# Delta rule: two merge columns moved from behind the early heads into a front pair, and a later ready mark for the conversions

## The chip, the cores and the metric

The kernel runs on one core of one Trainium2 chip. The metric is the device time of one execution in microseconds (us). The time before is 2187.66 us, the median of three runs between 2187.45 and 2188.29. A program on one core has TensorE (matrix products, with its weight loads), VectorE (DVE), ScalarE (ACT), GpSimd (POOL) and SyncE (SP, which issues most DMAs).

## The reference, cut to what matters

One layer of an encoder works on 640 tokens (512 of a prompt, 8 times 16 of samples), in float32:

```
z = x @ w_in              # q|k|v|forget|gate (FoX), q|k|v|decay|beta|gate (delta rule), m_a, m_b
branch A: forgetting attention, 8 heads of 128        -> y_a = (o_a * silu(gate_a)) @ w_out_fox
branch B: causal convolution of width 4 and SiLU on q|k|v, l2-normalised q and k,
          gated delta rule, 8 heads of 128, in chunks -> y_b = (o_b * silu(gate_b)) @ w_out_gdn
h  = (sigmoid(m_a) * y_a + sigmoid(m_b) * y_b) @ w_out
x1 = layer_norm(alpha * x + h)
out = x1 + sigmoid(x1 @ w_pl_gate) * rms_norm(p @ w_pl_proj)
```

The change concerns the projection for `m_a` and `m_b`, here called merge columns: 32 blocks of 128 output channels, each 2048 deep, of which only the hyperbolic tangent is stored until the end (tensor `md`). It also concerns the delta rule of branch B, which runs head after head.

## The kernel before, in words

Every weight block of 128 channels is a "column". Weights and activations are split into a high and a low float32r part (tiles `wh`, `wl`, `xh`, `xl`), and a product is three matmuls: high by high, high by low, low by high. The 640 tokens are cut into two halves of 320.

There are two ways to compute a column. `column` (its matmuls in `mm6`, lines 396 and 397) runs 16 steps along the depth, each with six matmuls of 320, so 96 matmuls; `mcol` (line 1547 applies the tanh, line 1548 stores to `md`) does this for one merge column. `pair` (matmuls at line 474) takes two columns at once with seven products of half the depth, each of 8 steps of three matmuls: 168 matmuls for two columns. It needs sums of the weight blocks, made on DVE in `w_sum` (line 319), sums of the activations that are made once in `front`, and additions of the products (line 483 and in the closing functions such as `merges`, lines 1410 and 1414).

The program has stages: `front` (first columns, then `PAIRS` pairs: gates, values, `FRONT` merge columns, q and k of the heads in `APART`), `phase_fox` (attention, with the three merge columns that are left between and behind its heads, and the projection of p), `phase_gdn` (the delta rule), and `tail`.

In `phase_gdn` the main flow is, for every head h, three columns q, v, k, each evacuated by `strip_evac` (lines 844 to 849), and then `FILL[h]` merge columns. The fills carry no dependency on the head; they keep TensorE at work while the delta rule of earlier heads goes on. The last of them (two of `FILL[7]`) are written out separately, behind them follow four plain columns of `w_out_fox` and four half-depth pairs, then `until(gdone == 7)`, and `tail`, whose first column needs the output of head 7 as its last operand (`nop[15]`).

The order of all instructions is fixed at build time. The main flow calls `tick` once per step of six matmuls, and `tick` lets the side "lanes" take a step; a lane is a queue of generators, run one after another. A `yield n` in a lane means that it goes on after n ticks and not before the modelled engine has ended what it emitted. Some lanes step at every second tick only (`every = 2`, set to 1 when the columns of head 7 are done). `until(cond)` ticks without emitting any column until `cond` holds. The engines then take their instructions strictly in this order, and semaphores make them wait where the model was wrong. The lanes of the delta rule are:

- `conv`: `conv_silu` (line 852): four taps (ACT line 860, DVE line 863), tanh (ACT line 869), and the last two operations on DVE (lines 873 and 878), after which `self.ready[c] = h` is set. Before the last two it waits for `done[c]`, so as not to overwrite what an earlier head still reads.
- `work`: `gdn` (line 883). Its first instruction waits in the order for `chdone >= h - 3` and for `ready` of all three; it then emits transposes on TensorE (lines 895 to 898 and 908), a load on SP (line 888), and more.
- `blocks`: `gdn_blocks`, the inversion of 32 by 32 blocks: two DMAs through memory (`lanes`, line 980), then 62 dependent operations on DVE (lines 986 and 988).
- `feeds`, and `chunks`: `gdn_chunks` with `gdn_pro` and `gdn_dec`, the recurrence itself. It begins with the load of the state on SP (line 1014) and ends with the store of the final state (line 1195). Only one head at a time is in this lane.
- `ends`: `gdn_out` (the output transposes at lines 1051 and 1055), which sets `gdone`. At the start of the stage this lane also holds `scale_e`, which must end before `gdn` of head 0 may start.
- `sums`: sums of later weights (DMAs at lines 291 and 301, GpSimd at line 295).

The host lays the weight blocks out in the order of use, from the same constants `FRONT` and `FILL`.

Of the kernel before, what the change touches and what calls it, by code (L numbers as in the profile page):

```python
# [52 lines left out]
class Kernel:  # L53
# [5 lines left out]


    PIECES = 5
    FRONT = 32 - 5 - 7
    NG = 8
    PAIR0, PAIRS = 6, NG + 2 + FRONT // 2 + 2
    BETWEEN = 6,
    APART = 3, 6
    FILL = 1, 1, 1, 1, 1, 0, 0, 4
    PLAIN = 4
    GATES = 6
    FREE = 0.5  # L70
# [781 lines left out]
    def conv_silu(self, strip, ct, h, c, dst):  # L852

        nc, tp = self.nc, self.taps
        nc.gpsimd.tensor_copy(out=self.tails[:, ct, 0:3], in_=strip[:, NPT:NPT + 3])
        nc.gpsimd.tensor_copy(
            out=self.tails[:, ct, 3:27].rearrange("p (b r) -> p b r", r=3),
            in_=strip[:, NPT + 3:SW].rearrange("p (b r) -> p b r", r=19)[:, :, 16:19])
        y = self.zt([P, SW], "cy")
        nc.scalar.mul(y[:, 0:CV], strip[:, 0:CV], tp[:, 4 * ct:4 * ct + 1])  # L860
        yield -1
        for i in range(1, 4):
            nc.vector.scalar_tensor_tensor(out=y[:, 0:CV], in0=strip[:, i:i + CV],
                                           scalar=tp[:, 4 * ct + i:4 * ct + i + 1], in1=y[:, 0:CV],
                                           op0=ALU.mult, op1=ALU.add)
            yield -1
        self.untapped -= 1
        th = self.zt([P, SW], "cth")
        nc.scalar.activation(th[:, 0:CV], y[:, 0:CV], AF.Tanh)
        yield 2  # L870
        while self.done[c] < h - (2, 1, 3)[c]:
            yield
        nc.vector.scalar_tensor_tensor(out=dst[:, 0:NPT], in0=th[:, 0:NPT], scalar=1.0, in1=y[:, 0:NPT],
                                       op0=ALU.add, op1=ALU.mult)

        def dv(x):
            return x[:, NPT + 3:SW].rearrange("p (b r) -> p b r", r=19)[:, :, 0:16]
        nc.vector.scalar_tensor_tensor(out=dst[:, NPT:T].rearrange("p (b r) -> p b r", r=16), in0=dv(th), scalar=1.0,
                                       in1=dv(y), op0=ALU.add, op1=ALU.mult)
        self.ready[c] = h  # L880
        yield

    def gdn(self, h, kq, v):
        nc, cb = self.nc, self.cb
# [376 lines left out]
    def front(self, work):  # L1261
# [70 lines left out]
        def parts(src, hi, lo):  # L1332
            nc.scalar.copy(out=hi, in_=src)
            nc.vector.tensor_tensor(out=lo, in0=src, in1=hi.bitcast(F32), op=ALU.subtract)
# [86 lines left out]
        def heads(x, hf, z, u=None):  # L1421
# [8 lines left out]

            def close(h=self.APART[n - self.NG - 2 - self.FRONT // 2]):
                if x == 0:
                    nc.scalar.mul(o, o, FOX_SCALE)
                nc.sync.dma_start(out=self.qkd[h, x], in_=m[x])
                if x:
                    nc.sync.dma_start(out=self.o["fk"][h], in_=m[x])
# [10 lines left out]
        for n in range(self.PAIRS):  # L1447
# [3 lines left out]
            def back(i, k):  # L1451
# [14 lines left out]
                if i == 6:  # L1466
                    hi, lo = self.op[2 * k]
                    parts(tiles[k // 3][:, (k % 3) * HALF:(k % 3 + 1) * HALF], hi[:, xb], lo[:, xb])
            self.pair(xf, gates if n < self.NG else vals if n < self.NG + 2 else merges if n < self.NG + 2 + self.FRONT // 2
                      else heads, back)  # L1470
            if n < self.NG:
                self.ng += 2
            elif self.NG + 2 <= n < self.NG + 2 + self.FRONT // 2:
                self.nm += 2
# [76 lines left out]
    def phase_gdn(self, conv, work):  # L1551
# [20 lines left out]
        for h in range(H):  # L1572
# [13 lines left out]
            work["gens"].append(self.gdn(h, kq, v))  # L1586
            for _ in range(self.FILL[h] if h < 7 else self.FILL[7] - 2):
                self.mcol("sg")
# [750 lines left out]
def _layout(a):  # L2339
# [13 lines left out]
          for g in range(1)]  # L2353
    nf = Kernel.FRONT
    m_ = iter(m[nf + 3:])
# [13 lines left out]
    for h in range(H):  # L2369
        bl += [gq[h], gv[h], gk[h]]  # L2370
        bl += [next(m_) for _ in range(Kernel.FILL[h])]
    for n in ("w_out_fox", "w_out_gdn"):
# [78 lines left out]
```

## Time and profile before

| | us |
|---|---|
| median of three runs | 2187.66 (2187.45 to 2188.29) |
| the profiled execution | 2189.74 |
| its span, first to last instruction | 2188.0 |
| TensorE busy | 2162.9 |
| VectorE / ScalarE / GpSimd busy | 1526.9 / 1001.8 / 393.4 |
| mean granted TensorE clock | 0.996 |

The profile is one execution, read by the hardware profiler. Busy time of an engine sums the time in which at least one of its instructions ran; a matmul row gives a duration of about 310 ns, but matmuls overlap, so the pace is read from the start of one to the start of the next. "Idle before" is the time that an engine stood still ahead of an instruction, and the name behind the arrow is what released it. `SPq` is the queue of DMA issues on SP. The chain that ended last follows the work back from the last instruction. By the trace, `phase_gdn` reaches its first evacuation at 960.1 us and its last stores of half-depth pairs a little before 1660 us.

### The profile page before, as it was taken

To read this page: it belongs to the slowest core of one execution; us is meant where nothing else is said; L and a number is where in the kernel's file an instruction comes from. 1 tells how busy PE (TensorE), PEld (TensorE's weight loads), DVE (VectorE), ACT (ScalarE), POOL (GpSimd) and SP (SyncE) were. 2 spreads that over 40 slices of the span, in tenths; PEclk is the share of its full clock that TensorE was granted. 3 is DMA by queue.
4 is the path that set the end of the run, shared out by engine and by line. 5 is a ranking of instruction groups with operands and counts; after the bars stand their busy time and mean duration, and the time that the engine had idled before them with its cause. 6 is when DMAs were issued, how large, how long until landed. Compare 5 with 4: busy or idle time off the path is not lost.

```text
span 2188.0 us, 41906 instructions
## 1 busy us (share of the span) xinstructions
PE 2162.9 (99%) x15510; PEld 2094.9 (96%) x15510; DVE 1526.9 (70%) x3158; ACT 1001.8 (46%) x2198; POOL 393.4 (18%) x599
## 2 busy tenths in 40 slices
PE   9999999999999999999999999999999999999998
PEld 7799999999999999999999999988999999999998
DVE  6877786767765445575767567766657787789987
ACT  4344443444443333445555666554344343354544
POOL 0023232322200111013334333331000000011100
PEclk9999999999999999999999999999999999999999
DMA  6356556665549888579888888877467656574465
GB/s 233 103 184 198 188 185 204 203 202 183 185 157 339 279 277 293 199 254 284 199 195 194 184 193 189 188 174 205 143 235 255 222 164 208 195 272 135 148 229 172
DMA packets 236781, 451.07 MB, mean 206 GB/s; under 512 B 35416, under 2 KB 119000, under 8 KB 236576
## 3 DMA queue, kind: packets, MB, share of 16 engines
q1 hardware_dynamic: 220448, 419.02, 58.9%
q0 software_dynamic: 16128, 29.37, 8.2%
q8 instruction: 122, 2.00, 0.4%
q14 instruction: 83, 0.68, 0.1%
HBM read 353.22 MB, written 95.07 MB: 205 GB/s over the span
## 4 chain that ended last, share of the span: by engine, by line
PE 91%; DVE 3%; DMA 3%; ACT 1%; issue 1%; SPq 0%; POOL 0%; DVEq 0%; ACTq 0%
PE g L474 40%; PE g L396 20%; PE g L397 20%; PE g L440 2%; PE s L956 1%; PE s L778 1%; PE s L693 1%; PE s L734 1%; ACT wh L329 1%; DMA lanes<-ld 1%; PE s L1102 1%; PE s L440 0%; PE s L788 0%; DVE sx L986 0%; DVE sx L988 0%
## 5 line engine op out<-in xcount | busy, mean ns | idle before, releaser
L329 ACT CAST wh<-wr 128x512 fp32r<-128x512 f32 x630 | 384.9, 619 | 310.1 <-PE g L397 129.1
L335 DVE TENSOR_TENSOR wl<-wr,wh 128x512 fp32r<-128x512 f32 x518 | 362.0, 712 | 192.9 <-ACT wh L329 187.2
L474 PE MATMUL g<-xh,wh 128*128 128x320 f32 (+1 forms) x1200 | 373.6, 311 | 2.1 <-ACT m L1255 1.6
L474 PE MATMUL g<-xl,wh 128*128 128x320 f32 (+1 forms) x1200 | 371.8, 310 | 0.6 <-DVE xl L371 0.6
L474 PE MATMUL g<-xh,wl 128*128 128x320 f32 (+1 forms) x1200 | 371.9, 310 | 0.0
L396 PE MATMUL g<-xh,wh 128*128 128x320 f32 (+1 forms) x1056 | 347.3, 329 | 0.6 <-ACT wh L329 0.6
L396 PE MATMUL g<-xl,wh 128*128 128x320 f32 (+1 forms) x1056 | 327.8, 310 | 4.6 <-DVE xl L371 4.6
L397 PE MATMUL g<-xh,wh 128*128 128x320 f32 x1056 | 327.7, 310 | 0.0
L396 PE MATMUL g<-xh,wl 128*128 128x320 f32 (+1 forms) x1056 | 327.2, 310 | 0.0
L397 PE MATMUL g<-xl,wh 128*128 128x320 f32 x1056 | 327.2, 310 | 0.0
L397 PE MATMUL g<-xh,wl 128*128 128x320 f32 x1056 | 326.9, 310 | 0.0
L295 POOL TENSOR_TENSOR ws<-ws 128x171 f32<-128x171 f32 (+2 forms) x164 | 120.7, 736 | 634.6 <-DMA ws<-in_w 627.3
L474 PE MATMUL g<-t,wh 128*128 128x320 f32 (+1 forms) x1040 | 230.6, 310 | 0.0
L474 PEld LDWEIGHTS g<-xh,wh 128*128 128x128 f32 x1200 | 226.0, 188 | 3.6 <-ACT m L1255 2.1
L474 PEld LDWEIGHTS g<-xl,wh 128*128 128x128 f32 x1200 | 225.7, 188 | 1.2 <-DVE xl L371 1.1
L474 PEld LDWEIGHTS g<-xh,wl 128*128 128x128 f32 x1200 | 226.1, 188 | 0.0
L396 PEld LDWEIGHTS g<-xh,wh 128*128 128x128 f32 x1056 | 199.5, 189 | 13.3 <-issue 8.2
L396 PEld LDWEIGHTS g<-xl,wh 128*128 128x128 f32 x1056 | 199.6, 189 | 5.6 <-DVE xl L371 5.6
L397 PEld LDWEIGHTS g<-xh,wh 128*128 128x128 f32 x1056 | 199.8, 189 | 1.3
L397 PEld LDWEIGHTS g<-xl,wh 128*128 128x128 f32 x1056 | 199.4, 189 | 0.0
L396 PEld LDWEIGHTS g<-xh,wl 128*128 128x128 f32 x1056 | 199.2, 189 | 0.1
L397 PEld LDWEIGHTS g<-xh,wl 128*128 128x128 f32 x1056 | 199.1, 189 | 0.0
(440 smaller groups left out, 3958.5 us busy)
## 6 DMA issues: line engine op xcount, KB each, us to landing
wr<-in_w SPq DMA_DIRECT2D x255, 512.0 KB, 4.4
wl<-in_w POOLq DMA_DIRECT2D x112, 256.0 KB, 5.6
kc<-in_kc SPq DMA_DIRECT2D x32, 512.0 KB, 7.3
vc<-in_vc SPq DMA_DIRECT2D x32, 512.0 KB, 6.5
ws<-in_w SPq DMA_DIRECT2D x104, 128.0 KB, 2.7
sr<-in_w SPq DMA_DIRECT2D x22, 512.0 KB
md<-m SPq DMA_DIRECT2D x32, 320.0 KB, 3.2
t<-md SPq DMA_DIRECT2D x32, 320.0 KB
```

The costliest lines, as they stand in the source:

```text
L295: nc.gpsimd.tensor_tensor(out=o, in0=x, in1=y, op=op)
L329: nc.scalar.copy(out=hi, in_=src)
L335: nc.vector.tensor_tensor(out=lo, in0=src, in1=hi.bitcast(F32), op=ALU.subtract)
L396: nc.tensor.matmul(ps[0], whl[w], xhl[o][:, a], start=(first and x == 0), stop=(last and x == 2))
L397: nc.tensor.matmul(ps[1], whl[w], xhl[o][:, b], start=(first and x == 0), stop=(last and x == 2))
L440: nc.tensor.matmul(ps, x[:, sl], w, start=(s == 0 and n == 0), stop=(s == 15 and n == 2))
L474: nc.tensor.matmul(ps, a[:, w], b, start=(k == 0 and n == 0 and not more), stop=(k == last and n == 2), skip_group_check=True)
L693: nc.tensor.matmul(s1[32 * j:32 * j + 32, :], self.qpad[:, 2 * j + par, :], kc[:, (j % 2) * NPT:(j % 2 + 1) * NPT], start=(par == 0), stop ...
L734: nc.tensor.matmul(od[32 * j:32 * j + 32, 0:P], self.ppad[:, c, 2 * j + par, :], vc[:, o:o + P], start=False, stop=(par == 1 and c == 3), ...
L778: nc.tensor.matmul(ops[:, 0:P], vn[:, kb, :], pT[:, kb * P:(kb + 1) * P], start=(kb == 0), stop=(kb == i))
L956: nc.tensor.matmul(pp[:, o:o + 256].rearrange("p (a b) -> p a b", a=2), kq[:, 0, x], kq[:, :, x], start=True, stop=True)
L1102: nc.tensor.matmul(p[:, 0:2 * P].rearrange("p (a b) -> p a b", b=P), kt[g, 4, :], vm[g], start=True, stop=True)
```

## The change

```diff
     PIECES = 5
-    FRONT = 32 - 5 - 7
+    FRONT = 32 - 3 - 7
     NG = 8
     PAIR0, PAIRS = 6, NG + 2 + FRONT // 2 + 2
...
-    FILL = 1, 1, 1, 1, 1, 0, 0, 4
+    FILL = 0, 0, 0, 0, 1, 1, 1, 4
...
                                        in1=dv(y), op0=ALU.add, op1=ALU.mult)
+        yield 2
         self.ready[c] = h
-        yield
```

`FRONT` goes from 20 to 22, so `front` runs 23 pairs instead of 22; the added one is a pair of merge columns. `phase_gdn` then has seven merge columns instead of nine: heads 0 to 3 have none behind them, heads 4, 5 and 6 one each, head 7 four as before. In `conv_silu` the mark `ready` is set two ticks after the last operation was emitted instead of at once, and the generator ends there instead of one tick later.

## Prediction

> **What bounds the kernel now.** I read the page first, then the chain of work that ended last, then busy times by stage, TensorE's waits, and last the instructions around the places where TensorE stands still.
>
> ```profile
> span 2188.0 us, 41906 instructions
> ...
> PE 2162.9 (99%) x15510; PEld 2094.9 (96%) x15510; DVE 1526.9 (70%) x3158; ACT 1001.8 (46%) x2198; POOL 393.4 (18%) x599
> ```
>
> ```profile
> 107.88 217.03 PE g L474 x1476
> ...
> 362.44 281.94 PE g L474 x1918
> ```
>
> TensorE is busy for 2162.9 of 2188.0 us, and in the chain its matmuls of 320 follow each other without a gap: 217.03/1476 = 0.1470 us each, 281.94/1918 the same. So the time is the number of matmuls times 0.147 us, plus the places where TensorE waits. By stage (start and end, length, then busy time of TensorE, its weight loads, VectorE, ScalarE and GpSimd, granted clock, DMA share):
>
> ```profile
> 107.90:648.00 540.10, 538.85 (x3670) 538.24 (x3671) 392.08 (x524) 227.83 (x428) 140.90 (x144) 1.00 0.60 189
> ```
>
> ```profile
> 955.00:1540.00 585.00, 575.78 (x4328) 553.27 (x4327) 387.89 (x1180) 324.42 (x872) 188.65 (x323) 0.99 0.82 203
> ```
>
> ```profile
> 1450.00:1480.00 30.00, 25.89 (x201) 23.34 (x200) 23.47 (x85) 13.56 (x44) 6.24 (x9) 0.89 0.59 151
> ...
> 1510.00:1540.00 30.00, 25.59 (x201) 23.15 (x198) 21.07 (x55) 11.77 (x29) 1.73 (x5) 0.89 0.55 184
> ```
>
> The pair stage lacks 1.25 us of matmuls; the delta-rule stage lacks 9.2, nearly all in the last two stretches. TensorE's own waits from 955 to 1990 us name them (total, times, longest):
>
> ```profile
> PE g L396 <- DVE xl L371: 4.4, 2, 3.2
> PE s L895 <- DVE kqs L873: 4.4, 2, 4.1
> ```
>
> The second is the one the later ready mark speaks to: the first transposes of `gdn` came to the head of TensorE's queue before the conversion at line 873 had run. VectorE and TensorE there, and the same transposes one head earlier:
>
> ```profile
> 1442.09 1.81 DVE L863 SCALAR_TENSOR_TENSOR cy<-strip,taps,cy 128x664 f32<-128x664 f32 x2
> 1452.42 0.41 DVE L986 TENSOR_TENSOR sx<-sx,lanes 80x248 f32<-80x248 f32 x1 [8.53 <-DMA lanes<-ld]
> ...
> 1454.08 0.68 DVE L873 SCALAR_TENSOR_TENSOR kqs<-cth,cy 128x512 f32<-128x512 f32 x1
> ```
>
> ```profile
> 1454.90 1.09 PE L895 MATMUL s<-cb,kqs 128*128 128x128 f32 x4 [4.11 <-DVE kqs L873]
> ...
> 1456.29 0.62 PE L396 MATMUL g<-xh,wh 128*128 128x320 f32 x1
> ...
> 1459.37 0.47 PE L397 MATMUL g<-xh,wl 128*128 128x320 f32 x1
> ```
>
> ```profile
> 1396.26 0.60 PE L895 MATMUL s<-cb,kqs 128*128 128x128 f32 x4
> ...
> 1397.03 0.39 PE L1166 MATMUL s<-S,kqs 128*128 128x128 f32 x2
> ```
>
> VectorE stood for 8.53 us at the head of the block inversion of head 6, whose DMA was late, with the conversion of head 7 queued behind it. TensorE lost 4.11 us; then the transposes took 1456.29 - 1454.90 = 1.39 us against 0.77 one head earlier (+0.62), and twelve matmuls start 3.08 us from first to last instead of 11 x 0.147 = 1.62 (+1.46). Stall A costs 6.2 us in all.
>
> **The change, part by part.**
>
> *Products.* Two columns are 2 x 96 = 192 matmuls, 28.22 us; a pair is 7 x 8 x 3 = 168, 24.70 us. TensorE saves 24 x 0.147 = 3.5 us. The front grows by 24.7 us, the delta-rule stage loses 28.2 us of column work.
>
> *What the pair adds beside it.* Per pair four weight sums on VectorE and 14 high and low parts instead of 8:
>
> ```profile
> L335 DVE TENSOR_TENSOR wl<-sr,wh 128x512 fp32r<-128x512 f32 x174 | 126.3, 747 | 82.2 <-ACT wh L329 81.5
> ...
> L319 DVE TENSOR_TENSOR sr<-wr,sr 128x1024 f32<-128x1024 f32 x43 | 57.8, 1345 | 3.6 <-DMA sr<-in_w 3.6
> ```
>
> That is 4 x 1.345 + 14 x 0.747 = 15.8 us of VectorE, and with the additions 392.08/22 = 17.8 us per pair, beside 24.7 us of TensorE. The stage holds the 22 pairs of before and lacks 1.25 us of matmuls over all of them, so I cost it at nothing; uncovered, one sum would cost 1.3 us.
>
> *What leaves the delta-rule stage.* Eight conversions of weights, on ScalarE and GpSimd, which wait there for other things. By itself 0.
>
> *The later mark.* Two steps are 12 x 0.147 = 1.8 us. Behind it wait `gdn` of the same head in its lane and, one step longer than before, the next conversion; the main flow does not (it waits for the taps, counted before). A start of `gdn` delayed by 1.8 us costs at most that once at the end of the chain of heads. It gives back between 1.8 us (stall A at the same place, 4.11 - 1.8 left) and all 6.2. I take 6.2, since the start of head 7's `gdn` moves as well: it will wait for the recurrence of head 4, not for its own conversion.
>
> *The chain of heads.* This decides. The recurrence holds one head at a time. It begins with the load at line 1014 and ends with the store at line 1195; SP's issues, from several stretches:
>
> ```profile
> 1092.99 0.43 SPq L1014 DMA_DIRECT2D st<-in_st  x1
> ```
>
> ```profile
> 1431.17 0.42 SPq L1195 DMA_DIRECT2D out_stp<-S  x1
> ...
> 1441.92 0.33 SPq L1014 DMA_DIRECT2D st<-in_st  x1
> ```
>
> ```profile
> 1508.29 0.42 SPq L1195 DMA_DIRECT2D out_stp<-S  x1
> 1508.76 0.43 SPq L1014 DMA_DIRECT2D st<-in_st  x1
> ```
>
> ```profile
> 1586.08 0.38 SPq L1195 DMA_DIRECT2D out_stp<-S  x1
> 1586.52 0.45 SPq L1014 DMA_DIRECT2D st<-in_st  x1
> ```
>
> ```profile
> 1633.47 0.42 SPq L1195 DMA_DIRECT2D out_stp<-S  x1
> ```
>
> Eight recurrences fill 1092.99 to 1633.47, 540 us, 68 us each, against 42 us of own columns per head. Handovers take 0.4 us (1508.29, 1586.08); once, ahead of head 5, the lane stood for 10.75 us (1431.17 to 1441.92), because that head's last column was only evacuated at
>
> ```profile
> 1331.29 0.42 ACT L845 COPY strip<-g 128x320 f32<-128x320 f32 x1
> ```
>
> behind five fills. And at the end of the stage:
>
> ```profile
> 1649.08 4.43 PE g L474 x30
> ```
>
> ```profile
> 1652.43 0.35 DVE L1056 SCALAR_TENSOR_TENSOR og<-s,nwh,og 128x128 f32<-128x128 f32 x1
> ...
> 1657.62 0.83 DVE L371 TENSOR_TENSOR xl<-og,xh 128x640 fp32r<-128x640 f32 x1
> ```
>
> The last pair of the stage ends at 1653.5 us, the output of head 7 at 1652.8. Its low part is ready at 1658.45, and the tail's first column needs it at its eighth step, 7 x 0.88 = 6.2 us after 1653.5, at 1659.7. The slack is 1.2 us. So the columns and the chain of heads end together now, and 34.4 us off the columns (28.2 and stall A) are a gain only as far as the chain gets shorter too. Counted from the start of the stage, it loses for certain the 10.75 us (head 5 comes four fills earlier, so its `gdn` no longer waits for its columns) and the 6.2 us of stall A, which lay inside the recurrence of head 5: 17 us. The other 17.4 - 1.2 = 16 us must come from recurrences that run faster, or be waited for. What speaks for faster: the second-step pace of the lanes ends when head 7's columns are done, some 28 us earlier, and where columns run out nothing stands between the chain's steps on TensorE. The recurrence of head 7, with no inversion of another head on VectorE beside it, took 1633.47 - 1586.52 = 47 us against 78 for head 6 (1508.76 to 1586.08). What speaks against: heads 0 to 3 now come on 42 us of columns, so conversions and inversions are denser on VectorE. Bounds: 0 if the 16 us are all found, 16 if none. I take 5: two thirds found, as the uncovered rest runs at the chain's own latency.
>
> **Sum.** -3.5 - 6.2 + 5 = -4.7 us. Of the profiled execution's 2189.74 us that makes 2185.0; the median of the three runs is 2.1 us below that execution, so 2183.0 against 2187.66. From no change a measurement of this kernel can tell about 0.2%, 4.4 us.
>
> **Where a rule and a row part.** The stretch 1510 to 1540 us holds the waits of line 396, 3.2 us the longest and 4.4 in all, and has the granted clock of 0.89 that the stretch of stall A has. So I price a wait of some 3 us like stall A's 4.11: with 0.62 + 1.46 = 2.1 us of slow matmuls behind it. The Trainium skill ("TensorE: Matmul & The Clock Gate", "HAM oscillation — how this bites in real kernels") puts the limit at idle gaps over about 3.4 us; by it a wait of 3.2 us would have kept the clock, and the rival below in which such a wait comes back would be 2.1 us cheaper. The row speaks against it.
>
> **The rivals.**
>
> *The chain follows fully.* The 16 us are found, and the end costs nothing: -3.5 - 6.2 = -9.7, 2178.0. For it: the lane's last recurrence shows how fast one can be. Against: seven of eight run beside an inversion, before and after.
>
> *The chain does not follow, and the kernel is slower.* At the last `until`, in front of the tail, TensorE waits for head 7: the front is 24.7 us longer and the chain from the stage's start only 17 us shorter. That gives 24.7 - 17 = +7.7, less the 1.2 of slack: +6.5, 2194.2. It decides as soon as the recurrences are not faster by 9.7 us together. For it: handovers of 0.4 us, so the lane is full. Against: the uncovered rest would run with VectorE nearly free.
>
> *Stall A moves.* The inversion's DMA is late at another head, VectorE stands, and transposes or the splits for the plain columns wait: 3.2 us of waiting and 2.1 of slow matmuls come back. -4.7 + 5.3 = +0.6, 2188.3. For it: the wait of 8.53 us is that of a DMA, which the change does not touch. Against: the mark leaves 1.8 us more and most `gdn` starts will wait for the recurrence.
>
> *The mark does nothing* is possible too: if every `gdn` waits for the recurrence, all of stall A's gain is the fills'. It changes no number.
>
> **How the numbers follow.** Forecast (part of the 16 us waited for, 2179 to 2187) 0.40; full gain 0.20; chain too slow 0.25; stall moves 0.15. Faster by over 0.2% (below 2183.3): 0.23 of the forecast's 0.40, 0.20 of the full gain, 0.02 of the moved stall: 0.45. Within: 0.15 + 0.12 of the moved stall + 0.06 of the slow chain = 0.33. Slower: 0.02 and 0.01 from the first and the last case and 0.19 of the slow chain: 0.22. The range reaches from 2176 (full gain with the second standing place gone too, 2 us) to 2194.5 (the slow chain).
>
> **What would show it.** Right: 23 pairs, the matmuls of 320 fewer by 24; no wait at line 895 over 2 us; the delta-rule stage 20 to 30 us shorter; a wait or thinner TensorE in the last 30 us ahead of the tail. Recurrence of head 5 beginning within 1 us of head 4's end. Wrong: TensorE idle earlier, at `until` of the evacuations; VectorE waits on `lanes` with TensorE behind them; the handovers of the recurrence open again; the waits for the splits at line 396 growing.

## The result, and the profile after

The changed kernel is slower: 2197.14 us, the median of seven runs (2193.57 to 2200.76), against 2188.29 for the kernel before in the same rounds (2187.45 to 2192.46). The ratio is 1.0033, with a 95% interval of 1.0023 to 1.0043. The prediction had 2183.0 and a range up to 2194.5. The profile that follows is of the slowest of the seven, 2200.76 us; that of the kernel before is of one of 2189.74 us.

The page of the changed kernel, its first lines:

```profile
span 2199.0 us, 41889 instructions
...
PE 2163.2 (98%) x15486; PEld 2094.7 (95%) x15486; DVE 1539.8 (70%) x3177; ACT 1004.0 (46%) x2201; POOL 402.5 (18%) x595
```

There are 24 matmuls fewer, and TensorE is still busy for as long as before (2163.2 us against 2162.9). The span grew by 11.0 us, and 10.7 of them are time in which TensorE stands still: 2199.0 - 2163.2 = 35.8 us, against 2188.0 - 2162.9 = 25.1. The stretch of the 23 pairs is as predicted (start and end, length, busy time of TensorE, its weight loads, VectorE, ScalarE, GpSimd):

```profile
107.90:672.70 564.80, 563.14 (x3833) 562.11 (x3834) 408.16 (x546) 237.32 (x447) 146.70 (x144) 1.00 0.58 185
```

It is 24.7 us longer and lacks 1.66 us of matmuls (1.25 before), so the added pair costs nothing beside its products. The delta-rule stage is where the time went. TensorE's longest waits from 900 to 2000 us (total, times, longest; the first five rows):

```profile
PE s L1051 <- ACT ob L1046: 6.7, 1, 6.7
PE g L396 <- ACT xh L370: 4.1, 1, 4.1
PE s L1125 <- DVE m L1116: 2.4, 1, 2.4
PE s L1179 <- ACT vn L1176: 1.9, 1, 1.9
PE s L1133 <- ACT xx L1129: 1.6, 2, 1.1
```

The wait of 4.1 us at line 895 is gone. The waits for the splits at line 396, 4.4 us before, are still there (4.1 in the second row and 1.0 further down). New are waits for the recurrence itself (lines 1125, 1133, 1179) and, the longest, one for the output of the last head, in front of the tail. The last column matmul, those transposes, and the first matmul of the tail:

```profile
1654.30 0.31 PE L474 MATMUL g<-xh,wl 128*128 128x320 f32 x1
1661.32 1.35 PE L1051 MATMUL s<-cb,ob 128*128 128x128 f32 x4 [6.71 <-ACT ob L1046]
...
1662.62 0.61 PE L396 MATMUL g<-xh,wh 128*128 128x320 f32 x1
```

Before, the same transposes ran without a wait, with column matmuls behind them up to the tail:

```profile
1648.38 0.60 PE L1051 MATMUL s<-cb,ob 128*128 128x128 f32 x4
...
1653.20 0.31 PE L474 MATMUL g<-xh,wl 128*128 128x320 f32 x1
1653.35 0.32 PE L396 MATMUL g<-xh,wh 128*128 128x320 f32 x1
```

They moved by 12.9 us, and the end of the span by 11.0. These rows say where the 11.0 us are. The last column matmul starts 1.1 us later than before (1654.30 against 1653.20); with the stall of the prediction gone and 24 matmuls fewer it should have come 9.7 earlier by the prediction's prices. From it to the first matmul of the tail it is 8.3 us instead of 0.15, the wait and the transposes. The tail itself, from its first matmul to the end of the span, takes 536.4 us instead of 534.7, with slow matmuls at its start (a granted clock of 0.81 from 1660 to 1675 us). So 9.9 us are lost at the end, behind the wait for the last head's output, and the 9.7 us that the columns were to gain are lost inside the stage.

SP's issues for the first recurrence, the handover to head 5, and the end of the last recurrence:

```profile
1133.80 0.60 SPq L1014 DMA_DIRECT2D st<-in_st  x1
```

```profile
1455.37 0.35 SPq L1195 DMA_DIRECT2D out_stp<-S  x1
...
1459.16 0.42 SPq L1014 DMA_DIRECT2D st<-in_st  x1
```

```profile
1648.08 0.42 SPq L1195 DMA_DIRECT2D out_stp<-S  x1
```

The first recurrence starts 40.8 us later than before (1093.0), of which the longer front is 24.7: the remaining 16 us are new. `gdn` of head 0 loads its row (line 888) at 1040.5 us instead of 1013.6, so 13.9 of the 16 lie between that load and its recurrence. All eight, the time from the load at line 1014 to the store at line 1195 added up, take 507.5 us instead of 524.2, and the handovers together 6.8 instead of 16.3. So the chain of heads, counted from the start of the stage, is 24.7 + 1633.5 - 1648.1 = 10.1 us shorter by its last store, and 24.7 + 1648.4 - 1661.3 = 11.8 by the last transposes, where the stage lost 28.2 us of columns.

What held the last recurrence up is not only its own work. ScalarE stood for a load of weights with a step of the recurrence (line 1176) next in its order, and the wait of 1.9 us at line 1179 follows from it:

```profile
1635.79 0.62 ACT L329 CAST wh<-wr 128x512 fp32r<-128x512 f32 x1 [5.87 <-DMA wr<-in_w]
1636.31 0.36 ACT L1176 ACTIVATE vn<-s,cs 128x128 f32<-128x128 f32 x1
```

From 1590 to 1660 us such waits of ScalarE (line 329 for `in_w`) add up to 12.4 us here and to 3.9 in the kernel before. The last recurrence took 54.1 us instead of 47.0.

### The profile page after: what moved, and what is told of

The parts are those of the page before. It is cut to its first block, busy times and chain, and to the rows that moved or that the text cites. A ratio compares the mean times of both kernels' runs of the same rounds, so it can differ in the third digit from the quotient of the medians.

```text
span 2199.0 us, 41889 instructions
## 1 busy us (share of the span) xinstructions
PE 2163.2 (98%) x15486; PEld 2094.7 (95%) x15486; DVE 1539.8 (70%) x3177; ACT 1004.0 (46%) x2201; POOL 402.5 (18%) x595
## 5 line engine op out<-in xcount | busy, mean ns | idle before, releaser
L397 PE MATMUL g<-xh,wh 128*128 128x320 f32 x1024 | 318.3, 311 | 0.0
L397 PE MATMUL g<-xl,wh 128*128 128x320 f32 x1024 | 317.9, 310 | 0.0
L397 PE MATMUL g<-xh,wl 128*128 128x320 f32 x1024 | 317.3, 310 | 0.0
```

The source lines that it names most:

```text
L397: nc.tensor.matmul(ps[1], whl[w], xhl[o][:, b], start=(first and x == 0), stop=(last and x == 2))
```

## Experiments

Theory (T): the delta rule's chain of heads sets the end of its stage, and columns taken out of the stage are cover taken away. Rivals: the later mark costs by itself (A); the loss lies elsewhere (B); the place of the fills is what costs (C); for faster stepping, the engines' own latency sets the recurrences (D). One more rival has no run of its own: every edit shifts the order of all later instructions, and a shift can cost by itself. Ratios are against the kernel before in the same rounds on the same chip, with 95% intervals.

**The mark alone (e1).** The kernel before with

```
-        self.ready[c] = h
-        yield
+        yield 2
+        self.ready[c] = h
```

> The kernel before with the later ready mark alone; columns and fills unchanged. Theory (the chain of heads sets the end of the delta-rule stage, the mark does little): the wait of 4.11 us at line 895 and its 2.1 us of slow matmuls shrink by 1.8 to 6.2 us, and the chain does not get longer; 2182 to 2187 us. Rival A (the later mark delays every start of gdn and so lengthens the chain): slower than before by 5 us or more, with the wait ahead of the tail that the changed kernel has.

Measured: 2197.51 us, 1.0035 [1.0023, 1.0047]. The theory's number missed: the mark alone costs as much as the whole change. The waits of this kernel from 955 to 1990 us:

```profile
PE s L1051 <- ACT ob L1046: 5.5, 1, 5.5
PE s L1179 <- ACT vn L1176: 4.6, 1, 4.6
```

None is left at line 895, and the wait in front of the tail is there although no column left the stage. Again it is the last head's output that comes late. The store of the last recurrence is issued at 1655.2 us instead of 1633.5. Part of these 21.7 us is the store's own delay: the last step of the recurrence on VectorE (line 1184) runs at 1646.2 instead of 1631.0, 15.2 later, and the last transposes at 1658.2 instead of 1648.4, 9.8 later. The eight recurrences, by load and store, take 526.8 us, 2.6 more than before, but the handovers take 32.5 us instead of 16.3, half of that ahead of head 5:

```profile
1441.82 0.34 SPq L1195 DMA_DIRECT2D out_stp<-S  x1
...
1458.12 0.33 SPq L1014 DMA_DIRECT2D st<-in_st  x1
```

`gdn` of heads 2, 4 and 5 begins 8 to 9.5 us later than before (the loads at line 888: 1133.1, 1273.4 and 1346.0 us against 1124.0, 1265.6 and 1336.5), of the others by at most 2.7. Two steps are 1.8 us. Where the rest comes from was not isolated. ScalarE's waits for weights from 1590 to 1660 us are 12.9 us in this run.

**The moved columns alone (e2).** The kernel before with

```
-    FRONT = 32 - 5 - 7
+    FRONT = 32 - 3 - 7
-    FILL = 1, 1, 1, 1, 1, 0, 0, 4
+    FILL = 0, 0, 0, 0, 1, 1, 1, 4
```

> The kernel before with the moved columns alone (23 pairs, fills 0,0,0,0,1,1,1,4); the ready mark unchanged. Theory (the stage loses 28 us of column work, the chain of heads does not get shorter by as much, and the front is 24.7 us longer): as slow as the changed kernel, 2194 to 2200, with a wait of 5 us or more in front of the tail. Rival A (the mark is what costs): 2178 to 2184.

Measured: 2199.56 us, 1.0050 [1.0034, 1.0066], with the wait in front of the tail (5.4 us), as expected. (The profile is of the slowest of its six executions, 2208.54 us.) So A alone is out: the columns cost without the mark as well, and the two costs do not add up.

**A shorter chain (e3, e4).** In the changed kernel and in the kernel before, the inversion stops after 8 of 31 steps:

```
-        for j in range(31):
+        for j in range(8):
             n = 31 - j
```

> The changed kernel with the inversion cut from 31 to 8 steps (the last 23 eliminations of every block are left out, so 46 of 62 operations on VectorE per head). Theory (chain of heads): the recurrences start earlier and meet a freer VectorE, the wait of 6.7 us in front of the tail goes, and the time falls by 10 us or more, to 2178 to 2186. Rival B (the loss is in the front pair or in waits that the chain does not set): it stays above 2192.

> The kernel before with the same cut of the inversion, as the control. Theory (chain of heads): there the columns already cover the chain but for 1.2 us, so only single waits can go: 2180 to 2188, and the cut changed kernel is now 2 to 5 us faster than it, the 3.5 us of matmuls that the pair saves. Rival B: both fall alike, and the cut changed kernel stays some 9 us slower than this one.

Measured: the changed kernel falls to 2173.15 us, 0.9923 [0.9908, 0.9937], the kernel before to 2185.0, 0.9971 [0.9959, 0.9982]. Cutting the same work of the heads is worth some 24 us in the one, more than the range expected, and some 6 in the other. The last head's transposes in the cut changed kernel and in the cut kernel before:

```profile
1623.28 0.60 PE L1051 MATMUL s<-cb,ob 128*128 128x128 f32 x4
```

```profile
1624.06 0.60 PE L1051 MATMUL s<-cb,ob 128*128 128x128 f32 x4
```

They come without a wait, 13.0 and 24.8 us ahead of the tail's first matmul (1636.30 and 1648.82): here the columns set the end. With the chain out of the way the change is a gain of 11.8 us, where 2 to 5 were expected. In size that is near the full gain of the prediction (9.7), but not in its parts: the cut kernel before has only 1.7 us of waits at line 895. The 3.5 us of matmuls are in it; the rest is other waits and slow matmuls. The gain exists, but it needs a chain that is shorter than it is. The cut also shifts the order of the instructions, which these two runs do not separate.

**An earlier start of the chain (e9, e10).** `scale_e`, behind which `gdn` of head 0 waits, handles two rows a step and loads eight ahead instead of four, in the changed kernel and in the kernel before:

```
-        for n in range(4):
+        for n in range(8):
             load(n)
...
-            yield 2
+            if n % 2:
+                yield 2
```

> The changed kernel with the chain of heads started earlier: the scaling of the embedding rows (scale_e), which must end before gdn of head 0, does two rows per step instead of one and loads eight rows ahead instead of four; the same work in fewer steps, nothing left out. Theory (the chain of heads sets the end of the stage in the changed kernel): gdn of head 0 starts 8 to 14 us earlier after the stage's first column, the wait ahead of the tail of 6.7 us goes, and the time falls by 7 to 14 us to 2183 to 2190. Rival B (the end is set by something else, the start does not matter): 2195 to 2199.

> The kernel before with the same earlier start, as the control. Theory (chain of heads): there the third to sixth heads wait for their columns and columns and chain end together, so an earlier start moves the end little: 2184 to 2191. Rival B (the scaling itself costs time): it falls as much as the changed kernel does.

Measured: 2208.12 us, 1.0083 [1.0069, 1.0097], and 2202.99, 1.0061 [1.0045, 1.0078]. Both are far above every range expected. `gdn` of head 0 loads its row (line 888, three lines further down in this kernel) at

```profile
1040.75 0.43 SPq L891 DMA_DIRECT2D gr<-rd  x1
```

against 1040.5 us in the changed kernel. (In e10 it is 1.8 us earlier than in the kernel before.) So this says nothing on an earlier start. It does show how far the order alone moves the end: the same work in another order is half a per cent slower, in e9 than the changed kernel and in e10 than the kernel before. The last head's transposes come at 1673.5 and 1670.3 us, each behind a wait of 5.4 us in front of the tail (both profiles are of the slowest of six executions). An effect of this size is as large as that of the change itself. Why later heads got slower was not settled.

**The place of the fills (e5, e16).** The changed kernel with the first and with the second of

```
-    FILL = 0, 0, 0, 0, 1, 1, 1, 4
+    FILL = 1, 1, 1, 0, 0, 0, 0, 4
+    FILL = 1, 0, 0, 0, 0, 1, 1, 4
```

> The changed kernel with its seven fills as 1,1,1,0,0,0,0,4 instead of 0,0,0,0,1,1,1,4: same matmuls, same front, same mark. Theory (chain of heads, and crowding of the first heads makes it start late): the first recurrence begins 10 us earlier again, but heads 4 to 7 come as late as they did, so the end moves by less than 5 us: 2192 to 2200. Rival C (the place of the fills is what costs): 2180 to 2188.

> The changed kernel with the fill of head 4 put behind head 0 (1,0,0,0,0,1,1,4): same matmuls, front and mark. Theory (chain of heads, started late by the crowding of the first two heads): the first recurrence begins some 15 us earlier; the end moves only as far as the later recurrences do not give that back, 2186 to 2196. Rival F (the late start is harmless because later recurrences are shorter for it): 2195 to 2199, no change.

Measured: 2193.22 us, 1.0021 [1.0011, 1.0032], and 2199.64, 1.0040 [1.0027, 1.0054]; e16 is above the 2186 to 2196 us that I had expected. With a fill behind head 0 the first recurrence does start earlier, at 1118.3 us in e5 and 1127.2 in e16 against 1133.8. The last store is issued at 1648.1 us in e5, as in the changed kernel, and at 1657.4 in e16.

```profile
1118.33 0.49 SPq L1014 DMA_DIRECT2D st<-in_st  x1
```

```profile
1648.12 1.77 SPq L1195 DMA_DIRECT2D out_stp<-S  x1
```

The eight recurrences give back what the start gained, and in e16 more (521.2 and 524.2 us instead of 507.5). In these two runs start and recurrences trade against each other. With seven fills C is out for the bulk of the loss; the intervals of e5, e16 and the changed kernel overlap.

**The fills late, but nine of them (e6).** The kernel of e1 (the kernel before with the mark) with

```
-    FILL = 1, 1, 1, 1, 1, 0, 0, 4
+    FILL = 0, 0, 1, 1, 1, 1, 1, 4
```

> The kernel before (22 pairs, nine fills) with the later mark and the fills as 0,0,1,1,1,1,1,4: the move to later heads without taking columns out of the stage. Theory (chain of heads): the stage has its 28 us of cover back, the wait ahead of the tail is under 3 us and the time is 2184 to 2193, below the changed kernel. Rival C (empty early heads alone make it slow): 2195 or more.

Measured: 2190.86 us, 1.0000 [0.9991, 1.0009]. The same mark, with the 28 us of columns kept in the stage, is no slower than before. The wait in front of the tail is 5.4 us, though, not under 3 as I had expected. And e1 has the same mark, the same front and the same nine fills in other places, at 1.0035: with nine fills their place is worth as much as the whole loss of the change. So e6 does not show that it is the number of columns in the stage that counts. ScalarE's waits for weights from 1590 to 1660 us are 1.9 us in e6, against 12.9 in e1; whether that is the difference was not tested.

**Faster stepping (e11, e12, e13).** The lanes step at every tick from head 1 on, in the changed kernel, in the kernel before, and in e6:

```
-            if h == 7:
+            if h == 1:
                 self.every = 1
```

> The changed kernel with the lanes of the delta rule stepping at every tick from head 1 on instead of from head 7 on: same instructions, the chain of heads emitted in fewer steps of column work. Theory (chain of heads sets the end): the eight recurrences with their gaps take less than the 514 us of the changed kernel, the output transposes of head 7 come earlier by as much, and the time falls to 2177 to 2190. Rival B (the end is set by something else): within 3 us of the changed kernel. Rival D (the engines' own latency, not the steps, sets the recurrences): the chain is no shorter and TensorE waits inside it, 2195 to 2210.

> The kernel before with the same faster stepping, as the control. Theory: the columns end the stage there as well, so at most the single waits go: 2181 to 2189. Rival D: 2190 or more.

> Twenty-two pairs, nine fills as 0,0,1,1,1,1,1,4, the later mark, and the faster stepping from head 1 on. Theory: a shorter chain with the cover of before; 2178 to 2188, faster than the kernel before. Rival D: 2190 or more.

Measured: 2193.6 us, 1.0010 [1.0000, 1.0019]; 2207.89, 1.0074 [1.0058, 1.0090]; 2190.21, 0.9991 [0.9980, 1.0002]. All three miss the theory's range. In the changed kernel the recurrences shrink to 483.2 us and the time by a fifth of a per cent. The last head now waits for its own inversion:

```profile
1578.11 0.42 SPq L1195 DMA_DIRECT2D out_stp<-S  x1
1583.70 0.33 SPq L994 DMA_DIRECT2D xd<-sx  x1
...
1590.73 0.45 SPq L1014 DMA_DIRECT2D st<-in_st  x1
```

The recurrence of head 6 is over at 1578.1, the inversion of head 7 at 1583.7, and only then can head 7 begin. Even so its transposes (1654.2 us) stand without a wait, and the tail follows the last column directly at 1657.4, 4.0 us later than in the kernel before. So here the columns set the end, and what delays them are waits inside the stage: those at the recurrence's own matmuls (lines 1102, 1125 and 1174) add up to 12.5 us. e13 is alike. Its recurrences take 450.3 us, the last transposes come 9.2 us ahead of the tail, and the tail starts 2.1 us later than before, behind 10.5 us of waits inside the stage. A chain that ends in time is not enough: TensorE takes its instructions in order, so each step of the recurrence that is not ready holds the columns behind it. In the kernel before, without the mark, the faster stepping costs 16 us and the waits for the conversions are back:

```profile
PE s L895 <- DVE kqs L873: 9.6, 4, 7.0
PE s L1051 <- ACT ob L1046: 6.8, 1, 6.8
```

The changed kernel with the same stepping has none of the waits at line 895, as the mark intends.

**The other direction (e7, e14, e15).** One pair fewer in front than before and eleven fills, with the mark (e7) and without (e14):

```
-    FRONT = 32 - 5 - 7
+    FRONT = 32 - 7 - 7
-    FILL = 1, 1, 1, 1, 1, 0, 0, 4
+    FILL = 1, 1, 1, 1, 1, 1, 1, 4
```

and two pairs fewer and thirteen fills, with the mark (e15): `FRONT = 32 - 9 - 7`, `FILL = 1, 1, 1, 1, 2, 2, 1, 4`.

> The other direction: one pair fewer in front than before (21 pairs, FRONT 18), eleven fills as 1,1,1,1,1,1,1,4, with the later mark. Matmuls +3.5 us against before, the front 24.7 us shorter, the stage 28 us of column work longer. Theory (chain of heads): the chain no longer ends last, no wait ahead of the tail, the output transposes of head 7 come with time to spare; the time is set by the columns, 2184 to 2194. If taking columns out of the stage were a gain by itself (the opposite view), it would be 10 us or more slower than before.

> FRONT 18 and eleven fills (1,1,1,1,1,1,1,4) without the later mark. Theory (the mark costs only where the chain of heads ends last): with cover to spare it shows only in single waits at line 895, of up to 4 us, so 2178 to 2186, within 5 us of the same kernel with the mark (2180.4). Rival A (the mark lengthens the chain and costs by itself): 5 us or more faster than with the mark, 2170 to 2176.

> One pair fewer still: FRONT 16, thirteen fills (1,1,1,1,2,2,1,4), with the later mark. Theory: with FRONT 18 the columns already set the end, so the further cover is worth nothing and the pair's 24 matmuls cost 3.5 us: 2182 to 2187, 2 to 6 us slower than FRONT 18. Rival E (more cover keeps paying): below 2179.

Measured: 2180.44 us, 0.9946 [0.9929, 0.9964]; 2178.76, 0.9949 [0.9937, 0.9962]; 2187.25, 0.9982 [0.9973, 0.9991]. With 24 matmuls more than before the kernel is half a per cent faster, and e7 lies below the 2184 to 2194 us that I had expected. The last head's transposes stand directly in front of the tail, without a wait, so the time to spare that I had expected there is not shown. TensorE's waits from 900 to 2000 us in e7 are these three and no others:

```profile
PE g L474 <- ACT ob L1046: 2.0, 1, 2.0
PE g L474 <- DVE xl L371: 0.6, 1, 0.6
PE s L1102 <- DVE og L1052: 0.4, 1, 0.4
```

The page of e7:

```profile
PE 2160.2 (99%) x15534; PEld 2093.0 (96%) x15534; DVE 1512.0 (69%) x3135; ACT 999.6 (46%) x2199; POOL 408.6 (19%) x607
```

TensorE is busy for less time than before with more matmuls (2160.2 against 2162.9 us), because slow matmuls behind the waits are gone: the mean granted clock is 0.999 instead of 0.996. The recurrence now waits for heads, not the reverse:

```profile
1550.63 0.34 SPq L1195 DMA_DIRECT2D out_stp<-S  x1
1583.88 0.42 SPq L1014 DMA_DIRECT2D st<-in_st  x1
```

That is a lane standing for 33 us ahead of head 7. With the mark or without is the same here, so with eleven fills the mark costs nothing that shows. One pair fewer still is slower than e7 by 6.8 us, more than the 3.5 us of its matmuls and than the 2 to 6 expected. By number of fills, with the mark: 13 give 0.9982, 11 give 0.9946, 9 give 1.0000 (e6) or 1.0035 (e1), 7 give 1.0033 (the change), 1.0021 (e5) or 1.0040 (e16). Without the mark: 11 give 0.9949, 9 are the kernel before, 7 give 1.0050 (e2). Of the numbers tried, eleven is the fastest; below it the place of the fills and the order count as much as their number.

## Why the prediction was wrong, point by point

The forecast was -4.7 us: -9.7 for the columns (products and stall A) and +5 for the end. By the two profiled executions the columns came 1.1 us later, and the end cost 9.9. Both terms failed.

*Products.* Right: 24 matmuls fewer, the front 24.7 us longer, the pair hidden on the other engines.

*Stall A.* Right that it goes. Wrong to book 6.2 us for it as if nothing else would take its place: e1 removes the same stall and is 7 us slower. The other waits of the stage, ahead of the one in front of the tail, add up to 14 us, where the kernel before had 9.9 in all with the 4.1 of stall A among them. The sum of the prediction put new waits inside the stage at nothing.

*The later mark.* "At most that once", 1.8 us, was wrong with nine fills in the places of before: e1 put the last step of the last recurrence 15.2 us later and the last transposes 9.8. With eleven fills (e7, e14) the mark cost nothing.

*The chain of heads.* This step failed. The chain as the thing that decides the end was read rightly; the wait in front of the tail, and e3 with e4, show it. The number for the chain was wrong: 17 us shorter "for certain" and two thirds of the rest found. Measured were 10 to 12 us, and nothing beyond. The recurrences and their handovers did shrink, by 16.7 + 9.5 = 26 us, but the first of them began 16 us later within the stage. I had carried the time from the start of the stage to the first recurrence over unchanged, though the same paragraph says that heads 0 to 3 would make VectorE denser; that VectorE is what delayed it was not isolated. In e5 and e16 an earlier start was given back by longer recurrences, so the start alone does not make the end.

*The end.* I priced it at 5 us, as a wait. The wait is 6.7 us; with the transposes, which now stand alone in front of the tail, and the slow matmuls behind them it is 9.9.

*The rivals.* The slower one (chance 0.25, 2194.2) had the mechanism and the place, the last `until`; its +6.5 us are +8.9. Its bound was the better forecast: no credit for what an uncovered chain might do. That its number came so near is in part luck: its chain was 5 to 7 us too short, and the columns, which it let end 9.7 us earlier, ended 1.1 later. The handovers of 0.4 us, which said that the lane was full, spoke for it, and I weighed them too lightly.

*What would show it.* Of the signs, no wait at line 895 and thinner TensorE ahead of the tail came true. The stage, from its first evacuation, is 23.6 us shorter to its last column matmul but only 15.4 to the first matmul of the tail, where 20 to 30 were forecast. The handover to head 5 took 3.8 us instead of under 1.

What stays open: why the mark delays `gdn` of some heads by 8 to 9.5 us and not by its own two steps, why e9 and e10 made later heads slower, and why e6 is faster than e1. All would need the order of single steps compared, not only their times. Two rivals for the length of the chain are untested: the shift of the order itself, and the late loads of weights on ScalarE. The latter cannot be all of it, since e14 and the cut kernel before have 10.0 and 12.3 us of such waits and none in front of the tail.

## What to carry to other kernels

Work that hides a dependent chain is not worth its own time but the time that the chain would be uncovered: before moving it, read where the chain and its cover end, and if they end together, price the move by the chain, and add a term for the waits inside the stage that come in place of the old ones. Credit a chain only with what a row shows, and count it from its first link to its last, because an earlier or later first link can be given back in between. Where the order of instructions is fixed, run the same work in a second order before calling a cause shown. And try the opposite move: here a dearer way to compute the same columns was half a per cent faster than the kernel before.

## What the runs showed of the hardware that was not expected

TensorE's clock fell behind waits of about 2 us in some places and not in others. In the changed kernel, TensorE from 1380 to 1425 us in three stretches (the column behind GpSimd's is the granted clock), and the matmuls behind the wait:

```profile
1380.00:1395.00 15.00, 13.95 (x101) 13.70 (x99) 2.47 (x7) 4.29 (x10) 5.56 (x13) 1.00 0.82 188
1395.00:1410.00 15.00, 13.65 (x108) 13.30 (x108) 13.69 (x48) 13.18 (x50) 4.00 (x7) 0.77 0.69 186
1410.00:1425.00 15.00, 15.00 (x135) 14.02 (x134) 13.33 (x46) 9.68 (x22) 5.82 (x10) 1.00 0.79 167
```

```profile
1396.35 0.63 PE L1125 MATMUL s<-m,lt 32*32 32x32 f32 x16 [2.40 <-DVE m L1116]
...
1397.62 0.47 PE L396 MATMUL g<-xl,wh 128*128 128x320 f32 x1
1397.88 0.47 PE L397 MATMUL g<-xl,wh 128*128 128x320 f32 x1
```

Behind the wait of 2.4 us the matmuls follow each other at 0.267 us instead of 0.147, and the clock is back at 1.00 in the third stretch. A wait of 1.9 us, in the stretch below, kept it:

```profile
1630.00:1645.00 15.00, 13.12 (x94) 12.85 (x94) 7.00 (x14) 5.04 (x12) 0.00 (x0) 1.00 0.68 244
```

No sharp limit lies between the two. In e13 a wait of 1.88 us in a dense run of column matmuls was followed by a clock of 0.83, and in e4 one of 2.79 us among such matmuls by 1.00 (each wait, and the stretch around it):

```profile
1026.30 0.42 PE L396 MATMUL g<-xh,wl 128*128 128x320 f32 x1 [1.88 <-DMA wl<-in_w]
1025.00:1035.00 10.00, 8.70 (x49) 8.70 (x50) 6.84 (x28) 6.18 (x17) 3.22 (x6) 0.83 1.00 257
```

```profile
1634.61 0.38 PE L474 MATMUL g<-xh,wh 128*128 128x320 f32 x1 [2.79 <-ACT wh L329]
1630.00:1640.00 10.00, 7.21 (x50) 6.97 (x49) 5.18 (x9) 4.80 (x9) 0.00 (x0) 1.00 0.70 242
```

All waits of 2.85 us and more in these traces, from 700 us on, were followed by matmuls at the slower pace. So a wait of 2 to 3 us cannot be priced as free or as slow from its length alone. Slow matmuls are also why 24 matmuls fewer left TensorE busy for as long as before: they save 3.5 us, and the mean granted clock is 0.994 instead of 0.996, over 2199 us some 4 us.

The Trainium skill ("TensorE: Matmul & The Clock Gate", "HAM oscillation — how this bites in real kernels") puts the limit at idle gaps of about 3.4 us. These traces do not agree: the clock fell behind waits of 1.88 and 2.40 us; the measurement decides.
